# Three triangular solves that change layout through DRAM, and six gate blocks moved into a scan

## The chip, the cores and the metric

The kernel runs on one core of one Trainium2 chip. The time is device time in microseconds of one execution; the median of the runs counts. A profiled execution gives a trace of every instruction.

Engines are called PE (TensorE, matrix multiply; PEld is its weight load), DVE (VectorE), ACT (ScalarE), POOL (GpSimd) and SP (SyncE, which mostly issues DMAs). Each engine executes its own queue in order. A DMA is issued by one engine's queue (SP, ACT or POOL here) and moved by 16 shared DMA engines.

## The reference, cut to what matters

One layer of a hybrid block over 512 latent tokens and 256 context tokens, 1024 channels, float32. The part that matters here is the chunked gated DeltaNet with 8 heads of 128 and chunks of 64 tokens, in both directions:

```
kb = k * beta
m = where(strict, einsum('bhnid,bhnjd->bhnij', kb, k) * decay, 0)
t_inv = triangular_solve(eye + m, eye, left_side=True, lower=True)      # 64 x 64, per chunk and head
u = t_inv @ (v * beta);  w = t_inv @ (kb * exp(gc))
# scan over chunks, state S of 128 x 128 per head and direction:
v_new = u_i - w_i @ S
o_i = q_i @ S + a_i @ v_new
S = S * d_i + k_i^T @ v_new
```

Twelve chunks (four of context, eight latent), two directions and eight heads give 192 triangular matrices of 64 by 64. Beside it the layer has a Hyena branch, an RG-LRU branch, gates computed as `act(h @ w_in[...])` (32 blocks of 128 columns by 512 tokens: silu of z, and three sigmoid gates), a merge, and a feed-forward part.

## The kernel before, in words

**Stages.** The kernel runs once through: modulation and Hyena filter (0 to about 240 us), the RG-LRU with one family of gates, queries and decays, keys, Gram products with the triangular solves and the values (about 500 to 764 us), the DeltaNet scan (764 to 977), Hyena, merge, feed-forward. A float32 product is done as three matmuls of rounded parts (`mm3`, L173 to L175): hi x hi, hi x lo, lo x hi. So each weight tile of 128 by 1024 is loaded by SP (L168), split into a rounded part (L155 on ACT or L157 on POOL) and a rest (L160 on DVE or POOL).

**Order.** Instructions are written in program order; a planner then sets the order of each engine's queue from that order as priority and from its own estimate of when operands are ready. In the scan PE's order is pinned to the program's (`in_order((ET.PE,))`). Memory is given out by fixed byte offsets (`at(offset in KB, shape)`, and `ring`, which cycles through offsets); two tiles at one offset wait for each other.

**Gram and solve.** `gram` (L803) forms k k^T for pairs of chunks on PE, multiplies with the decays on DVE and writes the strict triangles: `M1[0]` and `M1[1]` for the chunks that one direction's scan needs first, `M3` for the rest of both. It also writes q k^T products to DRAM (L827) from a ring of two buffers, `atr`. Each of the three solves inverts 64 matrices of 64 by 64. It sees each as four blocks of 32: the two diagonal blocks (128 x 32 of them lie over the partitions) are inverted by substitution, the off-diagonal one comes from two small products.

- L839: four DVE transposes of 32 by 1024 bring the diagonal blocks from "row on a partition" (M) to "matrix on a partition" (N).
- L841, L842: POOL sets X to identities.
- L844 to L850: 31 rounds of one product (L847) and one subtraction (L849) on DVE over all 128 matrices.
- L853 to L859: six DVE transposes bring X back, into M and, for half of it, into N (called Wu).
- L862 to L879: per half, 32 matmuls of 32 by 32 (L873), a copy on ACT (L874), 32 matmuls (L877), a copy with sign (L878).
- L886, L893: SP stores the inverses to DRAM (`wad`), from which the scan loads them.

`run` (L931) interleaves generators in rounds and takes one entry of a work list every `EVERY` rounds: first the two solves of `M1` with 12 entries, then the solve of `M3` with the rest. The list alternates nine value entries (`value`: a projection of 512 and 256 columns with a convolution on ACT and DVE, L502 to L507; `value_out`: PE transposes and a store) and 12 gate blocks (`gate`: 24 matmuls of 512 columns, an activation on ACT, L594, and a store from SP, L595).

**Scan.** `step` (L996) takes one chunk of each direction: W = state products (L1025), a subtraction on DVE (L1029), the inverse (L1035), a copy on ACT (L1037) into the ring `rvr`, the state product (L1043) and its update on DVE (L1048), for latent chunks also the output (L1055). Two gaps per step, 24 in all, are filled on PE with halves of gate blocks: 12 blocks, one half (12 matmuls) in each gap, accumulated in PSUM bank 0. On DVE `mod_part` (L1068) accumulates rows of `w_mod` as they arrive, and `mod_sum` (L1076) reduces them on PE, in bank 0 too. Chunk loads, gate weights, rows of `w_mod` and gate stores are all issued by SP. Region offsets: the second solve's N and X lie at 180 to 188 KB; `rvr` has 180, 182, 184 and 194.

Of the kernel before, what the change touches and what calls it, by code (L numbers as in the profile page):

```python
# [17 lines left out]
P = 128  # L18
# [55 lines left out]
def tile_block(ctx: ExitStack, tc: tile.TileContext, I: dict, out: bass.AP, dbg=None, upto=99):  # L74
# [517 lines left out]
    def gate_store(z_, m, pg):  # L592
        th = ur([P, NL])
        act(th, pg, GATES[z_][1])  # L594
        load(gated[z_, m], th)  # L595
# [25 lines left out]
    NFILL = 12  # L621
# [180 lines left out]

    def gram(i, hf):  # L803
# [12 lines left out]
        for d in range(2):  # L816
            db = DB[d][i][:, hs, :]
            if i in first[d]:
                vtt(M1[d][:, first[d].index(i), hs, :], g_, db, op=ALU.mult)
            else:  # L820
                for c in range(2):
                    rc = slice(c * 64, c * 64 + 64)
                    vtt(M3[d * 64:d * 64 + 64, second[d].index(i), c, hs, :], g_[rc], db[rc], op=ALU.mult)
            if lat:
# [4 lines left out]
    vtr = nc.vector.transpose  # L829

    def solve(dirs, M, NX_, tmr, eng):
# [3 lines left out]
        tt_ = vtt if eng == "dve" else gtt  # L835
        for qd in range(4):
            b, d = qd % 2, dirs[qd // 2]
            rows_ = slice(qd * 32, qd * 32 + 32)
            vtr(N[rows_] if d == 0 else N[rows_].rearrange("p j i -> p i j"),  # L839
                M[rows_, :, b * 32:b * 32 + 32].rearrange("p a i -> p i a"))  # L840
# [3 lines left out]
        for j in range(31):  # L844
            r = 31 - j
            tmp = tmr([P, r, j + 1])
            tt_(tmp, N[:, j + 1:, j].unsqueeze(2).to_broadcast([P, r, j + 1]),  # L847
                X[:, j, 0:j + 1].unsqueeze(1).to_broadcast([P, r, j + 1]), op=ALU.mult)
            tt_(X[:, j + 1:, 0:j + 1], X[:, j + 1:, 0:j + 1], tmp, op=ALU.subtract)  # L849
# [3 lines left out]
        for qd in range(4):  # L853
            b, d = qd % 2, dirs[qd // 2]
            rows_ = slice(qd * 32, qd * 32 + 32)
            xi = X[rows_] if d == 0 else X[rows_].rearrange("p j i -> p i j")
            vtr(M[rows_, :, b * 32:b * 32 + 32].rearrange("p a i -> p i a"), xi)
            if b == d:
                vtr(Wu[rows_].rearrange("p a j -> p j a"), xi.rearrange("p i j -> p j i"))  # L859
# [21 lines left out]
    def solve_first(d):  # L881
        yield from solve((d, d), M1[d].rearrange("p t h i -> p (t h) i"),
                         [at(158 + 14 * d + 4 * i, [P, 32, 32]) for i in range(2)], ring(1, seq(166 + 2 * d, 1, 2)),
                         "dve")
# [744 lines left out]
```

## Time and profile before

| | us |
|---|---|
| median of 3 runs | 1701.33 (1699.63 to 1703.97) |
| profiled execution | 1699.04 |
| its span in the trace | 1696.9 |
| PE busy | 1554.4 |
| DVE busy | 1202.8 |
| ACT busy | 618.8 |
| POOL busy | 587.0 |

The span is what the trace covers; 2.1 us lie around it. Busy is the time in which an engine executes something; matmuls are pipelined, so a busy PE need not be PE at its peak. The granted clock (PEclk) is the share of TensorE's full clock in a stretch: 1.00 is 2.4 GHz, 0.50 is 1.2 GHz, and a value between is a mix of the two. In timelines the first two columns are start and duration in us, in brackets stands how long the engine sat idle before and what ended that.

### The profile page before, as it was taken

The numbers are of one execution on the slowest core, as the hardware profiler recorded it, in microseconds if no ns is written. First come the engines' busy times: TensorE is split into PE (matmuls) and PEld (weight loads), VectorE is DVE, ScalarE is ACT, GpSimd is POOL, SyncE is SP. The second block draws the span as 40 slices with busy tenths as digits, with TensorE's granted clock in tenths as the row PEclk, the third lists the DMA queues.
The fourth block names the chain that finished last, engine by engine and source line by source line (L and its number), as shares of the span: only waits on it lengthen the run. The fifth ranks groups of instructions, "written<-read, shape, count | busy, mean of one in ns | idle before, by whom it ended". The sixth has DMA issues, their size and how long they took to land. (4 is left out here: it accounts for less than half of the span.)

```text
span 1696.9 us, 23679 instructions
## 1 busy us (share of the span) xinstructions
PE 1554.4 (92%) x9176; PEld 1264.1 (74%) x9176; DVE 1202.8 (71%) x1756; ACT 618.8 (36%) x1014; POOL 587.0 (35%) x407
## 2 busy tenths in 40 slices
PE   6989989889999988987899999999999999999998
PEld 1657767668787766875687777778878788888876
DVE  4677798765655999553675566777665899989873
ACT  3447878753454222231111150332222433333311
POOL 3752444433535351221333313222321234333441
PEclk7989999989999998788999999999999999999999
DMA  8522222234534332467889646322452123232331
GB/s 304 183 93 69 81 74 70 98 111 136 166 108 135 117 92 90 124 196 190 243 238 247 220 173 229 112 87 86 157 191 89 63 87 99 95 104 93 106 112 50
DMA packets 93057, 225.66 MB, mean 133 GB/s; under 512 B 9963, under 2 KB 30699, under 8 KB 92176
## 3 DMA queue, kind: packets, MB, share of 16 engines
q1 hardware_dynamic: 92112, 217.86, 40.9%
q0 software_dynamic: 832, 6.29, 0.9%
q8 instruction: 72, 1.18, 0.3%
q14 instruction: 41, 0.34, 0.1%
HBM read 190.45 MB, written 33.66 MB: 132 GB/s over the span
## 5 line engine op out<-in xcount | busy, mean ns | idle before, releaser
L173 PE MATMUL bank<-region,region 128*128 128x512 f32 (+1 forms) x2032 | 761.4, 376 | 23.8 <-DVE region L507 7.6
L175 PE MATMUL bank<-region,region 128*128 128x512 f32 (+1 forms) x2032 | 755.4, 373 | 24.6 <-DVE region L160 21.3
L174 PE MATMUL bank<-region,region 128*128 128x512 f32 (+1 forms) x2032 | 756.9, 373 | 5.0 <-DVE region L439 2.9
L173 PEld LDWEIGHTS bank<-region,region 128*128 128x128 f32 x2032 | 389.5, 192 | 101.6 <-ACT region L539 9.0
L175 PEld LDWEIGHTS bank<-region,region 128*128 128x128 f32 x2032 | 389.7, 192 | 97.7 <-DVE region L160 27.8
L174 PEld LDWEIGHTS bank<-region,region 128*128 128x128 f32 x2032 | 390.3, 192 | 69.6 <-DVE region L439 4.9
L160 DVE TENSOR_TENSOR region<-region,region 128x1024 fp32r<-128x1024 f32 (+2 forms) x241 | 269.8, 1133 | 173.0 <-ACT region L155 94.9
L155 ACT ACTIVATE region<-region 128x1024 fp32r<-128x1024 f32 (+2 forms) x209 | 178.4, 865 | 427.4 <-PE bank L174 130.0
L160 POOL TENSOR_TENSOR region<-region,region 128x1024 fp32r<-128x1024 f32 (+1 forms) x64 | 155.3, 2431 | 251.2 <-ACT region L155 210.8
L157 POOL TENSOR_SCALAR region<-region 128x1024 fp32r<-128x1024 f32 (+1 forms) x96 | 113.0, 1178 | 337.8 <-PE bank L174 151.2
L1443 DVE SCALAR_TENSOR_TENSOR region<-bank,pc,region 128x441 f32<-128x441 f32 (+2 forms) x352 | 224.8, 688 | 4.3 <-ACT region L1432 0.7
L505 DVE SCALAR_TENSOR_TENSOR region<-bank,pc,region 128x511 f32<-128x511 f32 (+1 forms) x56 | 34.1, 630 | 51.1 <-ACT region L502 47.3
L1074 DVE SCALAR_TENSOR_TENSOR region<-region,cc,region 128x1024 f32<-128x1024 f32 x28 | 42.1, 1504 | 35.9 <-DMA region<-in_w_mod_dram 35.5
L1012 POOL TENSOR_TENSOR region<-region,region 128x512 f32<-128x512 f32 x32 | 45.8, 1460 | 38.3 <-DMA region<-rowd 37.3
L502 ACT ACTIVATE region<-bank,pc 128x512 f32<-128x512 f32 (+1 forms) x40 | 23.0, 597 | 96.2 <-PE bank L175 96.2
L1455 POOL TENSOR_TENSOR region<-region,region 128x512 f32<-128x512 f32 x22 | 34.3, 1560 | 66.1 <-DVE region L1443 52.2
L1048 DVE SCALAR_TENSOR_TENSOR region<-region,egl,bank 128x128 f32<-128x128 f32 x160 | 42.3, 340 | 19.2 <-PE bank L1043 19.2
L1025 PE MATMUL bank<-region,region 128*64 128x128 f32 x608 | 38.9, 287 | 9.4 <-DVE region L1048 9.3
L1025 PEld LDWEIGHTS bank<-region,region 128*64 128x64 f32 x608 | 35.9, 145 | 14.6 <-DVE region L1048 6.3
L1037 ACT ACTIVATE region<-bank 128x512 f32<-128x512 f32 x24 | 14.3, 598 | 88.1 <-PE bank L1035 87.7
L594 ACT ACTIVATE region<-bank 128x512 f32<-128x512 f32 x32 | 18.8, 587 | 70.1 <-PE bank L175 66.0
L1035 PE MATMUL bank<-region,region 64*64 64x128 f32 x384 | 28.3, 298 | 12.7 <-DVE region L1029 6.9
(286 smaller groups left out, 1697.1 us busy)
## 6 DMA issues: line engine op xcount, KB each, us to landing
region<-in_w_in_dram SPq DMA_DIRECT2D x97, 512.0 KB, 3.6
region<-in_w_mod_dram SPq DMA_DIRECT2D x48, 512.0 KB, 6.7
region<-in_ffn_up_dram SPq DMA_DIRECT2D x44, 512.0 KB, 3.5
region<-in_w_proj_dram SPq DMA_DIRECT2D x24, 512.0 KB, 3.7
region<-in_ffn_down_dram SPq DMA_DIRECT2D x22, 512.0 KB, 3.4
gated<-region SPq DMA_DIRECT2D x32, 256.0 KB, 2.1
region<-gated SPq DMA_DIRECT2D x32, 256.0 KB, 3.5
kdd<-region SPq DMA_DIRECT2D x16, 384.0 KB, 2.8
```

What stands on the lines that cost most here:

```text
L155: act(hi, raw, AF.Copy)
L157: nc.gpsimd.tensor_scalar(hi, raw, 1.0, 0.0, op0=ALU.mult, op1=ALU.add)
L160: (vtt if e_lo == "dve" else gtt)(lo, raw, hi.bitcast(F32), op=ALU.subtract)
L173: mmul(ps, lh, rh, start=start, stop=False)
L174: mmul(ps, lh, rl, start=False, stop=False)
L175: mmul(ps, ll, rh, start=False, stop=stop)
L1012: gtt(wq[d][:, hs], KQ[hf][:, :, chs[d] - 4], eg[:, hs].unsqueeze(2).to_broadcast([P, 4, 2, 64]), op=ALU.mult)
L1025: mmul(X[hf][rcs[d], h, :], wq[d][:, hf * 4 + h, kind], S[d][:, hf * 4 + h, :], start=(kind == 0 or h == 0), stop=(kind == 0))
L1048: stt(S[d][:, h], S[d][:, h], egl[:, d, c, i, h:h + 1], p3[hf][d][:, h % 4], op0=ALU.mult, op1=ALU.add)
L1074: stt(acc, w_, cc[:, k, 0:1], acc, op0=ALU.mult, op1=ALU.add)
L1443: stt(uv[:, ro, co], pv_[:, ri, ci], w[:, a * 3 + b:a * 3 + b + 1], uv[:, ro, co], op0=ALU.mult, op1=ALU.add)
L1455: gtt(uu[0], uu[0], uu[1], op=ALU.mult)
```

## The change

All three solves go a new way between "row on a partition" and "matrix on a partition".

- On the way in, `gram` stores each finished M tile to a DRAM tensor `md` (SP's queue), and a solve fetches four quadrants from it, 32 rows by 32 matrices by 32 columns, with an access pattern that puts a matrix on each partition. The first part of all three solves stands right behind Gram (`next(g_)`). For the direction where the stored block is transposed the substitution runs from the other end (`upper`), so that nothing has to be turned; in the mixed solve one half is turned by a copy on ACT.
- On the way out ACT copies X with the inner axes swapped into N, stores both to a DRAM tensor `xd` and fetches M's four quadrants and Wu's two from there, all on ACT's DMA queue (`hop`). No DVE transposes are left in the solves.
- The work list is nine value entries and then six gate blocks (NFILL 12 to 6), one entry every four rounds, nine in the first `run`. The other six gate blocks become halves in the scan: 36 halves in 24 gaps, one in each first gap of a step and two in each second.
- Gate stores in the scan are issued on ACT's queue, and `mod_sum` uses PSUM bank 1 instead of bank 0.

```diff
-    def gate_store(z_, m, pg):
+    def gate_store(z_, m, pg, store=load):
         th = ur([P, NL])
         act(th, pg, GATES[z_][1])
-        load(gated[z_, m], th)
+        store(gated[z_, m], th)
...
-    NFILL = 12
+    NFILL = 6
...
+    md, xd = dr.tile([3, P, 32, 64], F32, name="md"), dr.tile([3, 2, P, 32, 32], F32, name="xd")
...
             if i in first[d]:
-                vtt(M1[d][:, first[d].index(i), hs, :], g_, db, op=ALU.mult)
+                t = first[d].index(i)
+                vtt(M1[d][:, t, hs, :], g_, db, op=ALU.mult)
+                if hf:
+                    load(md[d, :, t * 8:t * 8 + 8, :], M1[d][:, t])
...
+                if hf:
+                    t = second[d].index(i)
+                    load(md[2, d * 64:d * 64 + 64, t * 16:t * 16 + 16, :], M3[d * 64:d * 64 + 64, t].rearrange("p c h i -> p (c h) i"))
...
-    def solve(dirs, M, NX_, tmr, eng):
+    def solve(n, dirs, M, NX_, tmr):
         N, X = NX_
-        tt_ = vtt if eng == "dve" else gtt
-        for qd in range(4):
-            b, d = qd % 2, dirs[qd // 2]
-            rows_ = slice(qd * 32, qd * 32 + 32)
-            vtr(N[rows_] if d == 0 else N[rows_].rearrange("p j i -> p i j"),
-                M[rows_, :, b * 32:b * 32 + 32].rearrange("p a i -> p i a"))
+        upper = dirs == (0, 0)
+        quads = [(qd % 2, dirs[qd // 2], slice(qd * 32, qd * 32 + 32)) for qd in range(4)]
+        for b, d, rows_ in quads:
+            load((N if upper or d else X)[rows_], md[n, rows_, :, b * 32:b * 32 + 32].rearrange("j a i -> a j i"))
+        if not upper and 0 in dirs:
+            act(N[0:64], X[0:64].rearrange("p j i -> p i j"), AF.Copy)
...
         for j in range(31):
             r = 31 - j
+            if upper:
+                to, row = slice(0, r), slice(r, 32)
+                of = r
+            else:
+                to, row = slice(j + 1, 32), slice(0, j + 1)
+                of = j
             tmp = tmr([P, r, j + 1])
-            tt_(tmp, N[:, j + 1:, j].unsqueeze(2).to_broadcast([P, r, j + 1]),
-                X[:, j, 0:j + 1].unsqueeze(1).to_broadcast([P, r, j + 1]), op=ALU.mult)
-            tt_(X[:, j + 1:, 0:j + 1], X[:, j + 1:, 0:j + 1], tmp, op=ALU.subtract)
+            vtt(tmp, N[:, to, of].unsqueeze(2).to_broadcast([P, r, j + 1]),
+                X[:, of, row].unsqueeze(1).to_broadcast([P, r, j + 1]), op=ALU.mult)
+            vtt(X[:, to, row], X[:, to, row], tmp, op=ALU.subtract)
...
         Wu = N
-        for qd in range(4):
-            b, d = qd % 2, dirs[qd // 2]
-            rows_ = slice(qd * 32, qd * 32 + 32)
-            xi = X[rows_] if d == 0 else X[rows_].rearrange("p j i -> p i j")
-            vtr(M[rows_, :, b * 32:b * 32 + 32].rearrange("p a i -> p i a"), xi)
+        act(N, X.rearrange("p j i -> p i j"), AF.Copy)
+        hop = nc.scalar.dma_start
+        hop(xd[n, 0], X)
+        hop(xd[n, 1], N)
+        for b, d, rows_ in quads:
+            there = int(not (upper or d))
+            hop(M[rows_, :, b * 32:b * 32 + 32], xd[n, there, rows_].rearrange("a j i -> j a i"))
             if b == d:
-                vtr(Wu[rows_].rearrange("p a j -> p j a"), xi.rearrange("p i j -> p j i"))
+                hop(Wu[rows_], xd[n, 1 - there, rows_].rearrange("a i j -> i a j"))
...
-    EVERY, NW1 = 3, 12
+    EVERY, NW1 = 4, 9
...
-    work = [w_ for p_ in zip(values, gates) for w_ in p_] + values[len(gates):] + gates[len(values):]
-    run([solve_first(0), solve_first(1)], work[:NW1])
-    run([solve_second()], work[NW1:])
+    work = values + gates
+    solves = [solve_first(0), solve_first(1), solve_second()]
+    for g_ in solves:
+        next(g_)
+    run(solves[:2], work[:NW1])
+    run(solves[2:], work[NW1:])
...
-    mm = Banks([0])
+    mm, mm1 = Banks([0]), Banks([1])
...
-            mp = mm([P, 8])
+            mp = mm1([P, 8])
...
-                mp = mm([1, 512])
+                mp = mm1([1, 512])
...
-        gate_store(z_, m, pg)
+        gate_store(z_, m, pg, nc.scalar.dma_start)
```

## Rows read from the trace of the kernel before

**Rows 1.** The page's first part: busy us, share of the span, instructions.
```profile
PE 1554.4 (92%) x9176; PEld 1264.1 (74%) x9176; DVE 1202.8 (71%) x1756; ACT 618.8 (36%) x1014; POOL 587.0 (35%) x407
```

**Rows 2.** Windows: stretch, length, busy us (instructions) per engine, clock, DMA share, GB/s.
```profile
core 0: us, PE busy (x) PEld busy (x) DVE busy (x) ACT busy (x) POOL busy (x), PEclk, DMA share, GB/s
561.00:764.00 203.00, 177.93 (x1439) 150.89 (x1438) 162.59 (x279) 57.41 (x91) 63.15 (x27) 0.85 0.41 127
...
674.60:725.85 51.25, 47.16 (x374) 39.98 (x373) 33.12 (x75) 12.58 (x22) 11.86 (x9) 0.73 0.41 124
...
764.40:957.00 192.60, 167.62 (x1774) 139.12 (x1774) 111.27 (x226) 26.56 (x45) 60.32 (x48) 0.95 0.82 223
```

**Rows 3.** VectorE's lines, 561 to 764 us: busy us, mean ns, idle before.
```profile
L847 DVE TENSOR_TENSOR region<-region,region 128x31 f32<-128x31 f32 (+15 forms) x93 | 35.5, 406 | 1.1
L849 DVE TENSOR_TENSOR region<-region,region 128x31 f32<-128x31 f32 (+15 forms) x93 | 34.5, 395 | 1.1
L839 DVE STREAM_TRANSPOSE region<-region 32x1024 f32<-32x1024 f32 x12 | 25.4, 2120 | 0.3
L857 DVE STREAM_TRANSPOSE region<-region 32x1024 f32<-32x1024 f32 x12 | 25.3, 2104 | 0.3
L859 DVE STREAM_TRANSPOSE region<-region 32x1024 f32<-32x1024 f32 x6 | 11.9, 1990 | 0.0
...
L826 DVE TENSOR_TENSOR region<-bank,region 128x256 f32<-128x256 f32 x7 | 2.9, 421 | 1.4 <-DMA wad<-region 1.3
```

**Rows 4.** VectorE's timeline, 560 to 740 us: start us, us, instruction.
```profile
583.53 0.43 DVE L826 TENSOR_TENSOR region<-bank,region 128x256 f32<-128x256 f32 x1
...
588.49 0.21 DVE L847 TENSOR_TENSOR region<-region,region 128x31 f32<-128x31 f32 x1
...
701.49 1.14 DVE L505 SCALAR_TENSOR_TENSOR region<-bank,pc,region 128x511 f32<-128x511 f32 x2 [16.06 <-ACT region L502]
...
722.03 1.13 DVE L505 SCALAR_TENSOR_TENSOR region<-bank,pc,region 128x511 f32<-128x511 f32 x2
...
725.17 0.21 DVE L849 TENSOR_TENSOR region<-region,region 128x60 f32<-128x60 f32 x1
...
725.64 0.19 DVE L849 TENSOR_TENSOR region<-region,region 128x31 f32<-128x31 f32 x1
...
736.43 2.09 DVE L859 STREAM_TRANSPOSE region<-region 32x1024 f32<-32x1024 f32 x1
```

**Rows 5.** TensorE's timeline: small matmuls of the second solve, then the scan.
```profile
751.04 2.11 PE L873 MATMUL bank<-region,region 32*32 32x32 f32 x61
...
761.86 1.91 PE L877 MATMUL bank<-region,region 32*32 32x32 f32 x32 [0.68 <-ACT region L874]
769.09 0.66 PE L1035 MATMUL bank<-region,region 64*64 64x128 f32 x2 [5.32 <-DMA region<-vd]
...
867.32 0.50 PE L173 MATMUL bank<-region,region 128*128 128x512 f32 x1
...
870.28 3.71 PE L1025 MATMUL bank<-region,region 128*64 128x128 f32 x64
```

**Rows 6.** DMA issues: out<-in, queue, count, KB each, median us to landing.
```profile
gated<-region SPq DMA_DIRECT2D x32, 256.0 KB, 2.1
kdd<-region SPq DMA_DIRECT2D x16, 384.0 KB, 2.8
...
wad<-region SPq DMA_DIRECT2D x16, 128.0 KB, 3.8
```

**Rows 7.** ScalarE's lines, 561 to 764 us.
```profile
L155 ACT ACTIVATE region<-region 128x1024 fp32r<-128x1024 f32 x17 | 18.0, 1056 | 19.6 <-PE bank L174 12.4 <-DMA wad<-region 3.2 <-issue 2.5
```

**Rows 8.** Waits, 764 to 960 us: engine, for whom: us, times, longest.
```profile
PE bank L1025 <- DVE region L1048: 9.3, 4, 5.9
...
PE bank L1087 <- ACT region L594: 1.4, 2, 0.7
```

**Rows 9.** Waits of SP's DMA queue, 764 to 960 us.
```profile
SPq L595 <- ACT region L594: 29.8, 10, 8.5
```

More of the change, by code (lines that the diff above doesn't have):

```diff
@@ L827, in gram @@
                 load(wad[d, i, :, 1, hf * 256:hf * 256 + 256], at_.rearrange("p h i -> p (h i)"))
-    vtr = nc.vector.transpose
-    def solve(dirs, M, NX_, tmr, eng):
+    def solve(n, dirs, M, NX_, tmr):
         N, X = NX_
-        tt_ = vtt if eng == "dve" else gtt
-        for qd in range(4):
-            b, d = qd % 2, dirs[qd // 2]
-            rows_ = slice(qd * 32, qd * 32 + 32)
-            vtr(N[rows_] if d == 0 else N[rows_].rearrange("p j i -> p i j"),
-                M[rows_, :, b * 32:b * 32 + 32].rearrange("p a i -> p i a"))
+        upper = dirs == (0, 0)
[4 more added lines that the diff above has]
+            act(N[0:64], X[0:64].rearrange("p j i -> p i j"), AF.Copy)
         nc.gpsimd.memset(X, 0.0)
@@ L881, in solve_first @@
     def solve_first(d):
-        yield from solve((d, d), M1[d].rearrange("p t h i -> p (t h) i"),
-                         [at(158 + 14 * d + 4 * i, [P, 32, 32]) for i in range(2)], ring(1, seq(166 + 2 * d, 1, 2)),
-                         "dve")
+        yield from solve(d, (d, d), M1[d].rearrange("p t h i -> p (t h) i"),
+                         [at(158 + 14 * d + 4 * i, [P, 32, 32]) for i in range(2)], ring(1, seq(166 + 2 * d, 1, 2)))
         for a, i in enumerate(first[d]):
@@ L888, in solve_second @@
     def solve_second():
-        yield from solve((0, 1), M3.rearrange("p t c h i -> p (t c h) i"),
-                         [at(180 + 4 * i, [P, 32, 32]) for i in range(2)], ring(1, seq(188, 1, 2)), "dve")
+        yield from solve(2, (0, 1), M3.rearrange("p t c h i -> p (t c h) i"),
+                         [at(180 + 4 * i, [P, 32, 32]) for i in range(2)], ring(1, seq(188, 1, 2)))
         for d in range(2):
```

## The prediction, made before the changed kernel was run

> **What bounds the kernel now.** I began with the busy times of the page [rows 1]: TensorE carries 92% and VectorE 71% of the span, so a change off VectorE pays only where VectorE sets the pace. The window table of the stretch that the diff edits says where that is [rows 2]: from 561 to 764 us VectorE is busy 162.6 of 203 us, while TensorE has 25 us without work and is granted 0.85 of its clock on the mean of stretches at 2.4 and at 1.2 GHz. In 674.6 to 725.85 us the clock is 0.73, so TensorE's busy time there is stretched.
>
> The table of VectorE's lines shows what it does in that stretch [rows 3]: 186 products and subtractions of the substitution (L847, L849), 35.5 + 34.5 = 70.0 us, and 30 block transposes (L839, L857, L859), 25.4 + 25.3 + 11.9 = 62.6 us. The VectorE timeline gives the order [rows 4]: the last Gram product ends at 583.96, the first substitution is at 588.49, the last ends at 725.83, the last transpose at 738.52; one 16.06 us gap before 701.49 waits for a value block that TensorE was still multiplying. TensorE takes the second solve's small matmuls from 751.04 (gate blocks stand before them) and ends them at 763.77 [rows 5]. The scan cannot pass its first step before: its ring `rvr` begins at offset 180, where the second solve's N lies. So in this stage the chain is VectorE, then the small matmuls, then the scan. In the scan the bound is TensorE: 167.6 of 192.6 us busy at 0.95 clock [rows 2].
>
> **The change, part by part.**
>
> *The way in.* The 12 transposes at L839 go. In their place Gram stores M to DRAM (12 stores of 256 KB) and each solve fetches four quadrants of 128 KB as 1024 runs of 128 bytes. No row shows runs of 128 bytes. The nearest are two stores [rows 6]: 256 KB in 2 KB runs lands in 2.1 us, 384 KB in 512-byte runs in 2.8. Over 16 engines that is 40 more runs and 8 KB more per engine for 0.7 us. If bytes cost everything, 128 bytes are 11 ns; if runs cost everything, a run is 17.5 ns; I take 15. The far ends are 8 ns, and 58 ns (2.8 us / 48, as if landing had no fixed part). One fetch is then 64 x 15 ns = 0.96 us of every engine, on a fixed part of at most 2 us.
>
> When does substitution start? The Gram products no longer have transposes between them; what paces them is the ring of two buffers for the attention products, whose store takes 3.8 us [rows 6]: the seven left at 561 us need some 3.5 x 4.2 = 15 us, to 576. The last M product comes a little earlier, 575; its store 2.1, then four fetches 2 + 4 x 0.96 = 5.8: first substitution at 583, against 588.49. With no hiding at all (all 12 fetches first, at 58 ns each) it would be 575 + 2 + 2 + 44 = 623.
>
> *Substitution.* The same 186 operations in the same shapes, 70.0 us. Into them fall the value convolutions, 722.03 to 725.17, 3.14 us each [rows 4]. VectorE reaches values sooner, as gates no longer stand between them; I count five of eight still to come: 15.7 us. No transposes stand in it. 583 + 70.0 + 15.7 = 669, against 725.83.
>
> *The way out.* L857 and L859 go; ACT copies X transposed (1.06 us by the 128x1024 copy [rows 7]), stores X and N (512 KB each; 6 us for both with the copy, from the store rows), waits, and issues six fetches (2 + 6 x 0.96 = 5.8): 12 us, between 9, and 28 at 58 ns a run. For the first two solves the substitution of the second solve, a third of the 70 us, 23, hides it. For the second solve it is exposed: 681. Queued behind these waits on ACT are value and gate evictions, up to some 8 us per solve; the first two come out near 583 + 47 + 16 = 646. By then the values should be out of TensorE: a gate block is two halves of 2.96 us [rows 5], 5.9; a value block has half as many columns again, 8.9; at most seven are left at 561, to 623. Four banks take gate blocks meanwhile, so I charge nothing; without that cover it is 8 us for each of the first two solves.
>
> *The small matmuls.* From 751.04 to 763.77 before, 12.7 us [rows 5]. 681 + 12.7 = 693.7 against 763.8: -70. TensorE can follow: 62 us of values, 36 of gates and 768 small matmuls at 2.11 / 61 us [rows 5], 27, end at 686 with no stall. But small matmuls are where the clock fell before (0.73 over 51 us, 14 us lost [rows 2]); I leave 4 us of this. -66.
>
> *Six gate blocks in the scan.* Half a block lasts 867.32 to 870.28, 2.96 us [rows 5]; twelve more halves are +35.5 us on an engine that is already the bound. They land in every second gap, after L1055, where TensorE waits for the state update: 9.3 us in all [rows 8], covered now. In six of these gaps a gate ends and the next starts in the same bank, so TensorE waits for the eviction, 0.7 us each by the row of L1087 [rows 8]: +4.2. Weights: six more loads on SP, six more splits on GpSimd and VectorE (about 1.2 us each), on engines with slack here. +35.5 - 9.3 + 4.2 = +30.4; between +20 (other idle covered too) and +42 (nothing covered, splits in the way).
>
> *Stores of gates from ACT's queue, another bank for the modulation sums.* SP waited 29.8 us in the scan for ten evictions before it could issue stores [rows 9]; loads behind them now go earlier. TensorE's only wait on a load is 5.32 us at 769.09 for values [rows 5]. With the gates' buffers (152 to 156, where the first value load lands) free sooner, I take -3; from 0 to -5. The sums in bank 1 wait for the state update instead of a gate eviction: 0, at most +1 us four times.
>
> **Where a rule speaks against it.** The store rows price a 128-byte run at 11 to 17.5 ns [rows 6]. The Trainium skill, "DMA: Bandwidth & Descriptors", Specifications, says transfers under 512 bytes fall below line rate because the DMA engine reads, modifies and writes; "VectorE: DVE Perf Modes", The three transpose paths, warns that a plain DMA used as a transpose is 19 times slower than the hardware path. No run here shows a sub-512-byte DMA of weight. By that rule a run of 128 bytes would cost as much as one of 512 or more; this is the second rival below, and the sum by it is 1681.
>
> **Sum.** -70 + 4 + 30.4 - 3 = -38.6 us. The profiled execution took 1699.0 (span 1696.9 and 2.1 around it): 1660.4. The median of the three runs is 2.3 above the profiled one: 1662.7; I say 1662.
>
> **Rivals.**
> 1. *The scan gives more back, or TensorE binds the solves.* For: the scan is at 87% TensorE, and the clock stays low when small matmuls mix with gates. Against: the work of both stages at full clock fits in the times above. Price: +12 us in the scan and 6 more in the solves: 1680.
> 2. *Short runs are dear.* A 128-byte run costs what a 512-byte run costs if bytes are the whole price, 45 ns [rows 6]. Ten fetches lie on the chain (four in, six out), 640 runs per engine: 0.64 us per ns, (45 - 15) x 0.64 = +19: 1681. Against: 48 runs plus everything fixed took 2.8 us.
> 3. *Slower than before.* The same place, but fetches collide with the weights and M stores on the same engines and short reads queue. It decides at 15 + 39 / 0.64 = 76 ns a run; at 90 ns the time is 1662 + 48 = 1710. For: nothing in the trace has such runs, and the stage's DMA share, 0.41 [rows 2], rises. Against: it is beyond even the 58 ns end.
> 4. *More gain.* The clock stays up (-4), the extra halves meet the lower end of +20 (-10), and two or three more convolutions fall before 583 (-8): 1640. Against: each of these needs an order of the queues that the trace of before does not show.
>
> **Chances.** Forecast (1648 to 1674) 0.48, rivals 1 and 2 together 0.28, rival 4 0.12, rival 3 0.08, about no change 0.04 (several small prices of 1 and 2 at once). The range reaches over 1, 2 and 4: 1636 to 1696. What can be told from no change is 0.3%, 5 us. Faster by more than that: 0.48 + 0.28 + 0.12 less 0.02 of rivals 1 and 2 at their dear end = 0.86; same 0.06; slower 0.08.
>
> **What would show it.** Right: first substitution near 583, last near 669; the last small matmul near 694; a fetch landing in 3 to 4 us; from there to the scan's end about 220 us against 193, with TensorE over 90%. Wrong: VectorE idle before its first substitution for more than 15 us; TensorE or ACT standing behind ACT's waits during the first two solves; small matmuls of the second solve starting after 700; gaps before L1025 that remain although each second gap holds two halves.

## The result and the profile after

Forecast: 1662 us (1636 to 1696), faster with a chance of 0.86. Measured: 1727.1 us median of four runs (1721.7 to 1732.8) beside 1702.7 for the kernel before; ratio 1.0146, 95% interval 1.0100 to 1.0192. The change makes the kernel slower, by 1.5%. The profiled execution took 1722.27 us, against 1660.4 in the sum: 61.9 us more.

The page's first part, after: VectorE has 57 us less work, TensorE's stayed what it was, within 4 us [rows 1].

```profile
PE 1558.5 (91%) x9176; PEld 1266.8 (74%) x9176; DVE 1146.1 (67%) x1732; ACT 622.6 (36%) x1012; POOL 577.0 (34%) x407
```

The windows after (columns as in [rows 2]): from 561 us to the last small matmul, and from the first state product of the scan to its last state update.

```profile
561.00:746.80 185.80, 148.09 (x1337) 125.09 (x1335) 101.91 (x250) 57.10 (x83) 40.95 (x15) 0.79 0.58 153
...
746.80:971.30 224.50, 194.70 (x1845) 161.89 (x1844) 119.27 (x233) 29.73 (x49) 72.07 (x59) 0.93 0.79 216
```

The same two stretches of the kernel before, 561 to 763.8 and 777.4 to 957.4:

```profile
561.00:763.80 202.80, 177.93 (x1439) 150.89 (x1438) 162.59 (x279) 57.21 (x90) 63.15 (x27) 0.85 0.41 126
777.40:957.40 180.00, 160.06 (x1731) 132.83 (x1730) 107.82 (x225) 25.37 (x43) 60.72 (x48) 0.97 0.82 223
```

TensorE had 12 gate halves, about 35 us, less to do in the stage, and yet the last small matmul comes only 17 us earlier, at 746.8 and not at 693.7: TensorE is idle for 37.7 us there (24.9 before) at a lower clock. That is 53.1 of the 61.9 us. The other 8.8 lie behind it. (The sum also left 4 us in the stage for the clock; counted there, the split is 49.1 and 12.8.)

VectorE did what was forecast, some 9 us late: its timeline after, first and last substitution (583 and 669 in the sum).

```profile
591.56 0.67 DVE L861 TENSOR_TENSOR region<-region,region 128x31 f32<-128x31 f32 x1
...
677.65 0.19 DVE L863 TENSOR_TENSOR region<-region,region 128x31 f32<-128x31 f32 x1
```

What TensorE waited for in the stage, after (us, times, longest), and the longest of these waits in its timeline:

```profile
PE bank L926 <- ACT region L927: 16.5, 2, 15.5
PE bank L889 <- ACT region L927: 10.5, 1, 10.5
PE bank L889 <- DMA region<-xd: 4.4, 1, 4.4
PE bank L926 <- DVE region L834: 2.9, 1, 2.9
```

```profile
638.36 1.60 PE L926 MATMUL bank<-ident,region 128*128 128x128 f32 x6 [15.47 <-ACT region L927]
```

L926 is the transposes of values on TensorE, L927 the eviction of what they leave in a bank. Why it was late is read from ACT's timeline: L867 is the turned copy, L869 and L870 the stores of X and N, L873 and L875 the fetches.

```profile
635.54 1.99 ACT L867 ACTIVATE region<-region 128x1024 f32<-128x1024 f32 x1 [11.62 <-DVE region L863]
637.92 0.38 ACT L927 ACTIVATE region<-bank 128x256 f32<-128x256 f32 x1 [0.40 <-DMA vd<-region]
...
656.02 1.06 ACT L155 ACTIVATE region<-region 128x1024 fp32r<-128x1024 f32 x1 [8.38 <-PE bank L174]
...
670.74 0.34 ACTq L869 DMA_DIRECT2D xd<-region  x1
...
680.28 0.38 ACT L927 ACTIVATE region<-bank 128x256 f32<-128x256 f32 x1 [5.49 <-DMA region<-xd]
680.45 0.94 ACTq L869 DMA_DIRECT2D xd<-region  x1
...
698.31 0.34 ACTq L870 DMA_DIRECT2D xd<-region  x1
...
702.92 0.33 ACTq L873 DMA_DIRECT2D region<-xd  x1
...
727.45 0.31 ACTq L875 DMA_DIRECT2D region<-xd  x1
```

Three things are to be seen. ACT stood 11.6 us at the first solve's copy, until VectorE was done with it, and the eviction for which TensorE waited stood behind the copy. The next solve's X was ready at about 656 and was stored at 670.7: four roundings of weights (L155) stood in front, each waiting for TensorE to give a buffer back. The second solve's X was stored at 680.5, its N at 698.3, and its last fetch was issued at 727.5, 50 us after the last substitution, where the sum had 12 for the whole way out, landing included.

TensorE's waits in the scan, before and then after (L1030 is GpSimd's scaling of queries and keys, L1047 the subtraction, L1066 the state update):

```profile
PE bank L1025 <- DVE region L1048: 9.3, 4, 5.9
PE bank L1035 <- DVE region L1029: 6.9, 5, 3.5
```

```profile
PE bank L1043 <- POOL region L1030: 10.9, 6, 3.0
PE bank L1053 <- DVE region L1047: 9.0, 2, 8.3
PE bank L173 <- ACT region L594: 3.1, 4, 0.8
PE bank L1043 <- DVE region L1066: 2.6, 1, 2.6
```

The short transfers themselves are cheap, after (KB each, median us to landing; queue, packets, MB, share of 16 engines):

```profile
md<-region SPq DMA_DIRECT2D x12, 256.0 KB, 2.7
xd<-region ACTq DMA_DIRECT2D x6, 512.0 KB, 2.9
region<-xd ACTq DMA_DIRECT2D x18, 128.0 KB, 4.6
region<-md SPq DMA_DIRECT2D x12, 128.0 KB, 4.5
...
q10 hardware_dynamic: 22176, 10.23, 2.3%
```

### The profile page after: what moved, and what is told of

Its sections match the earlier page's. It is cut to its first block, busy times and chain, and to the rows that moved or that the text cites. A ratio compares the mean times of both kernels' runs of the same rounds, so it can differ in the third digit from the quotient of the medians.

```text
span 1720.5 us, 23703 instructions
## 1 busy us (share of the span) xinstructions
PE 1558.5 (91%) x9176; PEld 1266.8 (74%) x9176; DVE 1146.1 (67%) x1732; ACT 622.6 (36%) x1012; POOL 577.0 (34%) x407
## 5 line engine op out<-in xcount | busy, mean ns | idle before, releaser
L160 DVE TENSOR_TENSOR region<-region,region 128x512 fp32r<-128x512 f32 (+2 forms) x247 | 276.3, 1131 | 243.2 <-POOL region L157 143.5
L155 ACT ACTIVATE region<-region 128x1024 fp32r<-128x1024 f32 (+2 forms) x203 | 172.1, 859 | 442.5 <-PE bank L174 150.5
L157 POOL TENSOR_SCALAR region<-region 128x1024 fp32r<-128x1024 f32 (+1 forms) x102 | 119.3, 1171 | 398.4 <-PE bank L174 256.9
L160 POOL TENSOR_TENSOR region<-region,region 128x1024 fp32r<-128x1024 f32 (+1 forms) x58 | 137.8, 2380 | 240.9 <-ACT region L155 192.1
L1030 POOL TENSOR_TENSOR region<-region,region 128x512 f32<-128x512 f32 x32 | 44.0, 1403 | 55.6 <-DMA region<-rowd 55.6
L1043 PE MATMUL bank<-region,region 128*64 128x128 f32 x608 | 45.4, 310 | 14.3 <-POOL region L1030 10.9
L1473 POOL TENSOR_TENSOR region<-region,region 128x512 f32<-128x512 f32 x22 | 34.3, 1559 | 66.1 <-DVE region L1461 52.2
L1043 PEld LDWEIGHTS bank<-region,region 128*64 128x64 f32 x608 | 41.2, 159 | 20.2 <-POOL region L1030 12.7
L1066 DVE SCALAR_TENSOR_TENSOR region<-region,egl,bank 128x128 f32<-128x128 f32 x160 | 42.4, 338 | 13.4 <-PE bank L1061 13.4
L1175 POOL TENSOR_TENSOR region<-region,region 128x512 f32<-128x512 f32 x8 | 11.1, 1383 | 88.3 <-DVE region L1159 88.3
```

What stands on the lines that cost most here:

```text
L155: act(hi, raw, AF.Copy)
L157: nc.gpsimd.tensor_scalar(hi, raw, 1.0, 0.0, op0=ALU.mult, op1=ALU.add)
L160: (vtt if e_lo == "dve" else gtt)(lo, raw, hi.bitcast(F32), op=ALU.subtract)
L1030: gtt(wq[d][:, hs], KQ[hf][:, :, chs[d] - 4], eg[:, hs].unsqueeze(2).to_broadcast([P, 4, 2, 64]), op=ALU.mult)
L1043: mmul(X[hf][rcs[d], h, :], wq[d][:, hf * 4 + h, kind], S[d][:, hf * 4 + h, :], start=(kind == 0 or h == 0), stop=(kind == 0))
L1066: stt(S[d][:, h], S[d][:, h], egl[:, d, c, i, h:h + 1], p3[hf][d][:, h % 4], op0=ALU.mult, op1=ALU.add)
```

## The experiments

"Gates in the scan" are the six moved blocks. Times by ratio to the kernel before, run beside each; columns 3 to 7 are read from the profiles, in us: start of the last substitution, of the last small matmul, of the scan's first state product and of its last update, and span. They are those of one execution each, which took 5 us less than the median in the changed kernel, and 7 more in e5 and e15.

| run | ratio (95%) | subst. | small | state | update | span |
|---|---|---|---|---|---|---|
| before | 1 | 725.6 | 763.5 | 777.4 | 957.1 | 1696.9 |
| after | 1.0146 (1.0100 to 1.0192) | 677.6 | 746.6 | 746.8 | 971.0 | 1720.5 |
| e1 gates in the scan only | 1.0113 (1.0069 to 1.0157) | 730.3 | 749.5 | 749.6 | 970.2 | 1722.8 |
| e2 layout only | 1.0047 (1.0019 to 1.0076) | 671.3 | 773.2 | 786.1 | 970.1 | 1707.7 |
| e4 scan stores on SP | 1.0116 (1.0078 to 1.0155) | 680.2 | 751.0 | 751.2 | 972.5 | 1722.2 |
| e5 way out on GpSimd's queue | 1.0082 (1.0050 to 1.0114) | 676.6 | 744.5 | 744.7 | 966.6 | 1718.8 |
| e7 before, no layout change | 0.9899 (0.9849 to 0.9949) | 659.9 | 750.1 | 763.1 | 943.4 | 1683.0 |
| e8 e1, no layout change | 0.9900 (0.9859 to 0.9940) | 646.2 | 695.1 | 708.3 | 931.5 | 1683.1 |
| e9 before, values first | 0.9956 (0.9934 to 0.9979) | 702.5 | 752.7 | 765.9 | 944.6 | 1692.5 |
| e10 nothing of solves on ACT | 1.0040 (1.0016 to 1.0065) | 683.0 | 741.7 | 741.8 | 954.6 | 1708.0 |
| e11 last way out on VectorE | 1.0113 (1.0073 to 1.0154) | 685.3 | 723.4 | 741.5 | 969.3 | 1723.2 |
| e12 the same, nothing else | 1.0138 (1.0109 to 1.0168) | 676.4 | 736.2 | 749.5 | 969.5 | 1720.1 |
| e13 e10, eight loads fewer | 1.0003 (0.9974 to 1.0032) | 679.6 | 739.3 | 739.5 | 947.9 | 1699.6 |
| e14 e11, three more queues | 1.0028 (0.9998 to 1.0057) | 677.9 | 714.7 | 722.6 | 950.0 | 1700.7 |
| e15 e14, splits on GpSimd | 1.0009 (0.9995 to 1.0023) | 675.6 | 712.5 | 720.1 | 956.7 | 1707.5 |
| e16 e14, gates in the stage | 0.9745 (0.9725 to 0.9765) | 681.6 | 734.9 | 742.3 | 915.8 | 1656.4 |

**e1, e2: one part each.** e1 is the kernel before with the lines of the diff from `NFILL` on that concern the gates, their list and the modulation sums; e2 is the changed kernel with those lines as before.

> The kernel before with only the gate part of the change: six gate blocks into the scan, values first in the work list, gate stores of the scan on ACT's queue, modulation sums in bank 1; the transposes on VectorE stay. Theory (the scan costs more than forecast, and the layout part is a gain that was half lost in ACT's queue): the stretch from the first state product to the last update grows by about 46 us, as in the changed kernel (196.5 to 242.9); the solve stage loses its 16 us wait for a value block and ends 0 to 16 us earlier: 1699 + 46 - (0 to 16) = 1729 to 1745. Rival (the layout part is the loss, the gate part costs the forecast +30 or less and shortens the stage by some 25): 1705 or below.

> The changed kernel with the gate part undone: 12 gate blocks in the solve stage in the old list, one entry every three rounds, the scan as before; only the layout part is left. Theory (layout is a gain, cut short by ACT's in-order queue): TensorE has 36 us more work in the stage than in the changed kernel, so the last small matmul comes at 735 to 755 against 763.8 before, the scan lasts about 196: 1675 to 1692. Rival (the round trip through DRAM costs more than the transposes wherever the gates stand): 1705 or above.

Both parts lose. e1 took 1722.6 us, between the theory and the rival: its stage ends 14 us earlier than before, but the stretch from the first state product to the last update grows by 41 us, and what follows by 13. e2 is the rival's case: VectorE is done 54 us earlier, and the last small matmul comes 10 us later than before. In e2 the last turned copy on ACT starts at 712.9, 42 us after the last substitution, and the last fetches go out at 753.9 and later (one line's instructions: count, min/median/max ns, first and last start):

```profile
L867 ACT ACTIVATE region<-region x3: 1967/1976/2057, 629.6 to 712.9; 128x1024 f32<-128x1024 f32 x3
...
L873 ACTq DMA_DIRECT2D region<-xd x12: 309/328/909, 635.0 to 753.9; - x12
```

So the way out is late in ACT's queue here too. Whether the trip itself is dear, e2 leaves open.

**e5, e4: one queue changed.** `hop = nc.gpsimd.dma_start`; and `gate_store(z_, m, pg)` in the scan.

> The changed kernel with the way out (two stores, six fetches per solve) issued on GpSimd's queue instead of ACT's. Theory (the fetches were late because evictions that wait for TensorE stood between them in ACT's queue): in the second solve the stretch from the last substitution to the last fetch falls from about 50 us to 12 to 20, the last small matmul from 747 to 705 to 725, and the time by 20 to 35 us: 1690 to 1705. Rival (TensorE sets the stage's end anyway, with small matmuls at half clock): the fetches come earlier but the last small matmul stays within 5 us of 747, 1718 to 1727. Rival (short runs are what is slow): the hop stays at 40 us or more.

> The changed kernel with the gate stores of the scan back on SP's queue. Theory (the scan's surplus is TensorE's extra work and late loads, not the stores' queue): ACT's 13 us of waits for stores move to SP, and the time stays within 6 us of 1724. Rival (stores on ACT's queue, which land after 9.0 us against 2.1, hold ACT's evictions and with them TensorE): 8 to 15 us faster, 1709 to 1716.

e5 lies between the cases: the time fell by 11 us (by the ratios), but the last small matmul came only 2 us earlier, as the first rival had it. The copy was still on ACT (the 15.5 us wait at L926 is in its trace too), and GpSimd's queue also has weight splits: the second solve's stores went out at 701. e4 shows no difference: the interval overlaps that of the changed kernel, as the theory had it.

**e7, e8: the layout for nothing.** Starting from the kernel before (e7) and from e1 (e8), the transposes are left out and nothing stands in their place: `N = M[:, :, 0:32]` and `Wu = X`. The instructions left are the same, the values they compute are others.

> The kernel before with the change of layout left out altogether: no transposes and no trip through DRAM, the substitution reads M's first 32 columns as they stand and the small products take X (other values, same instructions otherwise). It gives the most that a free layout change could bring. The forecast's reading (VectorE, then the small matmuls, is the chain): substitution ends near 665 and the small matmuls follow; TensorE's own 178 us from 561 allow 739: 25 us gained, 1677. Theory after the first runs (TensorE's and ACT's order set the stage's end; in the run with gates alone moved VectorE ended 52 us later than in the changed kernel and the last small matmul only 3): last small matmul at 750 to 765, time 1688 to 1703.

> The same left out of the kernel in which the six gate blocks are moved and VectorE's transposes stand. The forecast's reading: substitution ends near 660, TensorE's work of some 150 us allows 711, the last small matmul comes at 700 to 715 against 749.7: 1684 to 1690. Theory (order, not VectorE): the last small matmul stays at 730 to 750: 1704 to 1722; the difference to the changed kernel (746.9) is then what the trip through DRAM costs in this order.

e8 goes against my theory: with a free way in and out the last small matmul comes at 695.1, somewhat before what I had given as the forecast's reading (700 to 715). The window from 561 us to there and the subtractions of the substitution:

```profile
561.00:695.40 134.40, 132.22 (x1278) 114.68 (x1274) 85.92 (x246) 47.38 (x78) 32.74 (x19) 0.87 0.47 147
```

```profile
L845 DVE TENSOR_TENSOR region<-region,region x93: 177/358/728, 562.4 to 646.2; 128x31 f32<-128x31 f32 x6, 128x60 f32<-128x60 f32 x6, 128x87 f32<-128x87 f32 x6, 128x112 f32<-128x112 f32 x6
```

The sum had 693.7, but that the two agree is luck. In the sum VectorE ends at 669 and the way out and 12.7 us of small matmuls follow. In e8 VectorE ends at 646.2 and the last small matmul comes 49 us later, because TensorE is the bound: it is busy 132.2 of 134.4 us. What e8 comes near is the prediction's side sum, in which TensorE's own work ends at 686 with no stall. So about 695 is what TensorE's own work leaves with six blocks in the stage, at this clock.

TensorE is idle for 2.2 us there and 37.7 in the changed kernel (+35.5), and busy 132.2 and 148.1 us, at clocks of 0.87 and 0.79 (+15.9): these two are the 51.4 us between the two stage ends. (4.3 us of the 15.9 are 32 products of the scan's first step, L1053, which the changed kernel runs before its last small matmul and e8 after it.) e7, with twelve blocks in the old list, also gains 17 us, but its stage ends at 750, as my theory had it; its time lies between the two cases. How much of that end is the order of the list and how much the six blocks more, no run separates.

**e9: the order of the list alone.** `work = values + gates` in the kernel before.

> The kernel before with one line changed: the work list is nine values and then twelve gates, as in the changed kernel, with nothing moved into the scan and the transposes kept. Theory (order in the stage is worth more than VectorE's instructions): the 16 us wait of VectorE for a value block goes and the stage ends 5 to 16 us earlier: 1686 to 1698. Rival (TensorE's 178 us are the bound, in any order): within 5 us of 1701.

Faster by 0.44%, as the theory had it. The 16.06 us wait [rows 4] is gone, substitution ends 23 us earlier and the stage 11.

**e10 to e13: where in the changed kernel the stage is lost.** e10: `hop = nc.gpsimd.dma_start`, both turned copies by `nc.vector.tensor_copy`, `gate(*f, "act", "dve")`. e11: e10 with the second solve's way out by the six old transposes, `hop = load if n else nc.gpsimd.dma_start`. e12: the changed kernel with those six transposes only. e13: e10 without the first eight loads and products of `w_mod`.

> The changed kernel with nothing in ACT's queue that waits for a solve: the turned copies on VectorE, stores and fetches on GpSimd's queue, and the six gate blocks' second split on VectorE, so that GpSimd's queue is free for them. Theory (value evictions behind the turned copies cost TensorE 16.5 and 10.5 us, and the second solve's fetches 40 more): the 15 us wait of TensorE before 640 goes, the second solve's way out takes 12 to 18 us, the last small matmul comes at 700 to 718, time 1690 to 1702. Rival (small matmuls at half clock fill the time anyway): last small matmul at 735 or later, time 1712 or more.

> The changed kernel with the way out split: the second solve, with which the stage ends, comes back by VectorE's six transposes; the first two go through DRAM, on GpSimd's and SP's queue, with their turned copies on VectorE; the gates' second split on VectorE. Theory (the fetches that end the stage wait in queues and in DMA traffic, transposes on an idle VectorE wait for nothing): substitution ends at 680 to 684, the transposes 13 us later, the last small matmul at 705 to 715 against 746.9, time 1680 to 1695. Rival (TensorE at half clock with its own work): last small matmul at 730 or later, time 1710 or more.

> The changed kernel with one edit: the second solve comes back by VectorE's six transposes, no turned copy, store or fetch of it; the first two solves stay as they are, on ACT's queue. Theory (of the 52 us that the stage ends later than forecast, the second solve's way out carries most): transposes end near 691, the last small matmul at 712 to 722, bounded by the first two solves' late fetches, time 1692 to 1705. Rival (the evictions behind the first solves' turned copies carry most): last small matmul at 735 or later, time 1712 or more.

> The run with copies on VectorE and the way out on GpSimd's queue, with the first eight rows of w_mod (512 KB each, 4 MB, the first of the scan) left out, so that their sum is zero. In that run the second solve's stores took 9 to 13 us and its fetches 8.7, at a DMA share of 0.98. Theory (they wait behind the scan's early loads): stores in 4 to 6 us, fetches in 4 to 6, the way from the last substitution to the last fetch 34 us before, now 18 to 24, last small matmul 741.9 before, now 722 to 734. Rival (the queue of GpSimd alone is what is late): stores as long as before, last small matmul within 4 us of 742. The total also loses eight products of 1.28 us on VectorE.

All four of my numbers for the stage were too good; by the last small matmul e10, e12 and e13 are the rivals' cases, and e11 misses the theory too (723.4, and with 1719.7 us the rival's time). e12 says that the second solve's way out alone is worth 10 us of stage and nothing in time; the waits for the eviction L927 stay at 16.7 and 10.5. From 690 us to its last small matmul TensorE is busy 42.3 of 46.4 us there: after its stalls in the first two solves it has enough left to do to end late by itself. e10 takes the 10.5 away and leaves 8.9 of the other: ACT now stood for value stores that SP issued late. In e13 the fetches land in 4.4 instead of 8.7 us, yet the stores stay at 11.6 and the stage ends 2.4 earlier: traffic was not the main price. e11 ends the small matmuls at 723.4, but the scan starts 18 us later, because its first loads stand in SP's queue behind stores that wait for ACT (SP's timeline of e11: L908 and L915 store the inverses, L1016 is the scan's first load):

```profile
707.41 0.79 SPq L908 DMA_DIRECT2D wad<-region  x2
...
716.08 0.80 SPq L908 DMA_DIRECT2D wad<-region  x2
...
721.53 4.00 SPq L915 DMA_DIRECT2D wad<-region  x3
725.63 0.64 SPq L1016 DMA_DIRECT2D region<-vd  x1
```

**e14: the queues put right.** e11, and (cut to what changes; `z_ < 3` are the gates of this stage):

```diff
-            load((N if upper or d else X)[rows_], md...
+            nc.gpsimd.dma_start((N if upper or d else X)[rows_], md...
...
-        gate_store(z_, m, pg)                       # in gate()
+        gate_store(z_, m, pg, nc.scalar.dma_start if z_ < 3 else load)
...
-                load(wad[d, i, :, 0, :].rearrange("(c j) x...   # solve_second
+                nc.scalar.dma_start(wad[d, i, :, 0, :].rearrange("(c j) x...
```

> The run with the split way out, with three more lists of DMAs taken off SP's queue: the fetches of the way in go to GpSimd's, the gate stores of the stage and the last solve's stores of inverses to ACT's. In that run ACT stood 7.4 to 8.9 us for value stores that SP issued late (fetches of the way in and weight loads that waited for buffers stood in front), and the scan's first loads were issued at 725.6, behind stores that waited for ACT. Theory (what is left of the loss is order in queues): TensorE's wait of 8.7 us before 640 falls under 3, the last small matmul comes at 700 to 714 against 723.6, the first state product at 715 to 728 against 741.5, time 1692 to 1708. Rival (what is left is the half clock of the small matmuls): last small matmul within 5 us of 723.6, time 1712 or more.

As the theory had it, to within a microsecond: 714.7, 722.6, 1703.6. No wait for L927's counterpart is left among TensorE's waits. Against e11, only who issues three lists of DMAs has changed: that is worth 9 us of the stage, 19 us of the scan's start and 14 of the time. Against the changed kernel e14 also has the last solve's six transposes, the turned copies and six weight splits on VectorE, and the way out of the first two solves on other queues (all in e11); together 20 us (1.0146 to 1.0028) are recovered. By the time alone e10 had 18 of these already (1.0040), with a stage only 5 us shorter than the changed kernel's: its scan, from the first state product to the last update, is 11 us shorter (213 against 224). e14 starts the scan 19 us earlier than e10 and ends it only 5 us earlier (227 long). Why the scan gives back what the stage gains, no run tells.

The stage of e14 still ends 21 us after the sum's 693.7, and along the sum's chain these can be found: the last transposes of the second solve (L872), and the two lines of small matmuls from 675 us.

```profile
L872 DVE STREAM_TRANSPOSE region<-region x2: 1855/1862/1870, 679.9 to 688.0; 32x1024 f32<-32x1024 f32 x2
```

```profile
L896 PE MATMUL bank<-region,region 32*32 32x32 f32 x256 | 15.1, 235 | 7.1 <-DVE region L872 7.1
L900 PE MATMUL bank<-region,region 32*32 32x32 f32 x255 | 14.8, 237 | 4.1 <-ACT region L897 4.1
```

The last substitution is 9 us late. The transposes end at 689.9, 12 us after it, which is the sum's price for the way out. Then the small matmuls take 25 us, not 12.7: 384 of them are still to come (256 in the kernel before, from 751.0), since those of an earlier solve stand beside the second solve's, and the clock is 0.50 (0.65 there).

**e15, e16: what remains is the gate part.** e15: `load_gate(z_, m, "pool", "pool")` in the scan. e16: e14 with `NFILL = 12`, `EVERY, NW1 = 3, 12`, and scan stores and bank as before.

> The last run (queues put right) with one edit in the scan: the rests of the gate weights are formed on GpSimd, which also rounds them, instead of on VectorE. In the last run VectorE stood 36.5 us in the scan for GpSimd's roundings, against 24.0 in the kernel before, and TensorE 14.7 us (once 11.2) for a subtraction of VectorE. Theory (the scan's idle time that was forecast to shrink by 5 and grew by 10 comes from VectorE's in-order wait for the six more splits): TensorE's wait for the subtraction falls from 14.7 to 5 or less, the stretch from the first state product to the last update from 227.7 to 212 to 220, time 1688 to 1697. Rival (TensorE's wait only moves, to GpSimd, which also forms the scaled queries, or to the loads): 224 or more, time within 5 us of 1703 or above.

> The queues put right, and the gate part undone: twelve gate blocks in the solve stage after the values, the scan as in the kernel before. Theory (TensorE's work is the same wherever the six blocks stand; in the scan they bring 10 us of new waits and 10 us behind it): the last small matmul at 740 to 752 against 714.7, the scan 180 to 184 long, the rest 739: 1680 to 1692, faster than the kernel before and than the one with only the order of the list changed (1694). Rival (the twelve blocks keep the small matmuls waiting as in the kernel before): last small matmul at 760 or later, 1698 or more.

e15 is the rival's case: TensorE's wait for the subtraction is 15.4 instead of 14.7, and VectorE, freed of the splits (36.5 us of waits in e14), now waits 70.8 us for rows of `w_mod`, 35.7 in e14. TensorE's and VectorE's waits in the scan, e14 and then e15:

```profile
PE bank L1060 <- DVE region L1054: 14.7, 4, 11.2
```

```profile
DVE region L160 <- POOL region L157: 36.5, 10, 7.8
DVE region L1099 <- DMA region<-in_w_mod_dram: 35.7, 9, 10.3
```

```profile
PE bank L1060 <- DVE region L1054: 15.4, 4, 7.8
```

```profile
DVE region L1099 <- DMA region<-in_w_mod_dram: 70.8, 15, 10.4
```

e16 beats both kernels and every theory: 1659.3 us, ratio 0.9745. Against e9, which has the same list but VectorE's transposes (1694.0 us), it is some 35 us faster: with its queues and splits put right the new way is a gain. Its windows: the stage, the end of the stage, the scan; then the same of e14.

```profile
561.00:734.90 173.90, 162.10 (x1415) 136.63 (x1413) 122.85 (x272) 57.72 (x90) 37.27 (x33) 0.94 0.65 183
675.00:734.90 59.90, 58.77 (x693) 49.24 (x692) 27.46 (x21) 19.94 (x29) 5.35 (x6) 0.87 0.64 192
742.30:916.10 173.80, 161.21 (x1731) 135.00 (x1730) 103.63 (x225) 25.37 (x43) 60.93 (x49) 0.96 0.87 237
```

```profile
561.00:714.70 153.70, 135.99 (x1289) 117.43 (x1289) 110.40 (x262) 47.05 (x77) 34.08 (x29) 0.85 0.58 159
675.00:714.70 39.70, 28.18 (x515) 26.95 (x516) 14.45 (x16) 9.74 (x17) 0.00 (x0) 0.52 0.39 107
722.60:950.30 227.70, 192.18 (x1843) 160.10 (x1843) 118.28 (x234) 29.04 (x48) 74.73 (x59) 0.93 0.79 213
```

Six blocks are worth 35 us of TensorE. In the stage they cost 20 (714.7 to 734.9): TensorE is idle 5.9 us less and busy only 26.1 us more. At the end of the stage, where e14 is idle for 11.5 of 39.7 us at a clock of 0.52, e16 is idle for 1.1 of 59.9 at 0.87. In the scan they cost 54 and behind it 10. (e16 also undoes the scan's stores on ACT's queue, for which e4 found nothing, and the bank, which no run changed alone.)

## Why the prediction was wrong, step by step

- **The way out** failed, and it is the main error: e8, without it, is 37 us shorter in span than the changed kernel, of 61.9 us. The sum had 12 us for the second solve and "I charge nothing" for ACT's queue during the first two, on the ground that the values would be out of TensorE by 623 and that four banks would cover. The values' projections were out, at 622.9, but not their transposes: TensorE stood from there for 15.5 us, because they needed a bank whose eviction stood behind the first solve's copy. I had priced this at 8 us per solve without the cover; the trace has 15.5 and 10.5. And I had taken the second solve's hop as a chain of copies and DMAs, without asking what the planner would put between its links. ACT stood for TensorE (27.8 us at L155 from 600 to 730), TensorE for ACT, and the hop for both: 50 us to the last fetch, at least 38 more than the sum had. e8 shows that without the trips the stage can end at 695. e11 and e14 bring back 32 of the 51 us between the changed kernel and e8, 9 of them by the issuing queues alone; e12 shows that the second solve's hop is not the whole of it, as the stalls during the first two keep the end late without it. The signs named in advance were there: ACT standing during the first two solves, and small matmuls after 700.
- **The way in and the substitution** were 8.6 us late, both by the same amount. The fetches landed in 4.5 us (3 to 4 in the sum), so their price was nearly right; the last product of M came at 582.3 (L828), and not at 575. The fetches of later solves went out until 630 us, two after each weight load that waited on SP: the same error in small, on another queue.
- **The small matmuls** were put next behind VectorE, at the 12.7 us that the second solve's took before. Their order was not fixed: in the changed kernel most of those of the first solves ran only from 681, beside those of the second. Where the way out is repaired (e14) this term is the largest that is off, 25 us. And with no trip at all (e8) it is not VectorE but TensorE's own work that ends the stage, which the sum checked with "no stall" and then left aside.
- **Six blocks in the scan:** TensorE's added work was +34.6 us (160.1 to 194.7; +35.5 in the sum). Its idle time was to shrink by 5 us and grew by 9.9 (19.9 to 29.8). The cover itself came: the waits for the state update fell from 9.3 to 2.6 us, and those for gate evictions are 3.1 where the sum added 4.2. What failed is the six loads and splits put at nothing, as "on engines with slack here": TensorE now waits 10.9 us for the queries and keys that GpSimd scales, for which it did not wait before, and 9.0 for VectorE's subtraction, 6.9 before. GpSimd in its turn stood 55.6 us for the `rowd` loads (37.3 before), and SP, which issues these, stood 29.9 us at loads of `w_mod` rows until VectorE's splits gave weight buffers back (4.3 before). Between the first state product and the last update the scan took 44.5 us more (180.0 to 224.5), and what follows 10 more, of which 4.7 are one wait for a weight's rounding on ACT (L155, 1.0 before) and about 3, by the sum's 2.96, the gate half more that stands in the last gap. Only 8.8 us of this show in the error, because the 13.6 us between the last small matmul and the scan's first state product (763.8 to 777.4) went too, which the sum did not foresee. In e8 they are there again, and its span, with no way out to pay, is still 24.8 us above the sum's (1683.1 against 1658.3): so large is this part of the error when the first is taken away. Which of the new waits is first, the runs leave open: e1, with the same blocks in the scan, has 0.5 us for GpSimd and 13.3 for the subtraction, and e15 moved VectorE's waits from the splits to the `w_mod` rows, which take the same ring of three weight buffers (`wr`) as gate weights. That SP's queue and this ring are the cause is what the waits point to; no run changed them alone.
- **Stores on ACT's queue in the scan:** -3 us in the sum; e4 shows no difference.
- **The rivals.** Dear short runs, at 45 ns or more, are refuted: the 2.3% of 16 engines over 1720.5 us are 633 us of engine time; if all of it went to the 18 fetches (18,432 runs of 128 bytes), a run took at most some 35 ns. Rival 1 was right for the scan: from the last small matmul to the end of the span the time grew by 40.6 us (933.1 to 973.7) where the sum had 27.4, and its price for this was 12. The slower side came true, but by another mechanism than the one I gave it; it had 0.08, and a queue that holds what others wait for was not among the rivals. The Trainium skill, "VectorE: DVE Perf Modes", The three transpose paths, states its 19 times for a large innermost stride in the destination. Here the innermost run is 32 values side by side on both ends, so no run of this case tests it. The Trainium skill, "DMA: Bandwidth & Descriptors", Issuing engines are not separate DMA queues, says that issuing from several engines saves only the time to initiate a DMA. Read as the whole price of a queue, it would make e14 against e11 worth a few issues of some 0.3 us. It was worth 9 us of stage and 19 of scan start, since what a queue costs here is not issuing but the wait of whatever stands in front.

## What to carry to other kernels

Price a moved transfer not by its landing but by the queue that issues it: list what waits in front of it and behind it on that engine, and for whom. A DMA that waits for another engine's result belongs on a queue with nothing behind it that the engines upstream need; where three lists must share two queues, keep one on the engine that is idle anyway, even if it costs more work (six transposes of 2 us here, which paid only together with the rest: e12 alone gained nothing in time). And before moving work from a stage with idle time into one that is bound by the same engine, sum its price in both: the same six blocks cost 20 us in one place and 64 in the other.

## What the runs showed of the hardware

- Where TensorE ran little but small matmuls (e14, 675 to 714.7 us, 11.5 us of it idle) its clock was 0.52, close to the lower of its two levels, and a product of 32 by 32 took 235 to 237 ns on the mean; in e16, where products of 512 columns run between them and 1.1 us are idle, the clock was 0.87 and they took 202 to 212 ns.
- A 128 KB fetch in 128-byte runs landed in 4.5 us from SP's queue and 4.6 from ACT's (after, medians). From GpSimd's it was 5.9 (e5), 6.9 (e10) and 4.4 (e13, with fewer loads beside it), so the queue alone does not set it. Issuing one took 0.79 us on GpSimd, 0.31 to 0.37 on ACT.
- The turned copy of 128 by 1024 took 1.94 us on ACT (1.06 in the sum, from a rounding of the same size) and 1.06 to 1.12 on VectorE (e10).
- The 512 KB stores of X and N landed in 2.9 us from ACT's queue (after, median of six) and in 5.4 from GpSimd's (e5), but the second solve's two in 11.4 and 11.6 from GpSimd's in e10 and e13, with and without the early `w_mod` rows; why, no run tells.
